# The last head group of a state space layer: gates first, its pairs moved amid another group's output, and the splits behind the transposes put first

## The chip, the cores and the metric

The kernel runs on one NeuronCore of a Trainium2 chip. The metric is device time of one execution in microseconds (us); lower is better. The kernel before takes 1437.23 us, the median of three runs (1435.54 to 1437.54).

## The reference

A two-layer encoder over 512 tokens of width 1024, in float32. The layer that the change touches is the second one, whose token mixer is a bidirectional state space scan:

```python
def ssd_mixer(hn, w_in, conv_w, conv_b, dt_bias, a_log, d_skip, norm_g, w_out):
    z, xbc, dt_raw = split(hn @ w_in)
    xbc = silu(depthwise_conv_centered(xbc, conv_w, conv_b))
    xs, bm, cm = split(xbc)
    dt = softplus(dt_raw + dt_bias)                   # per token, direction and head
    log_a = dt * -exp(a_log)
    y = bidir_scan(cm, bm, xs * dt[fwd], xs * dt[bwd], log_a[fwd], log_a[bwd])   # chunks of 128
    y = y + xs * d_skip
    y = y * silu(z)                                   # the gate
    yg = y by group (4 groups of 512 columns)
    yg = yg * rsqrt(mean(yg * yg) + EPS)              # RMS norm within the group
    return (yg * norm_g) @ w_out
```

In `bidir_scan` each head (32 heads of 64 columns, 8 to a group) needs a 128 x 128 matrix of decays per chunk, `exp` of differences of cumulative sums, times `c b` of its group. The layer then does `x = x + rms_norm(m)`, `hn = rms_norm(x)`, and a GeGLU feed-forward of which the up-projection comes first (`hn @ w_up`).

## The kernel before, in words

Every float32 matrix product is made as three products of a "high" and a "low" part (`mm3`, L86 to L88): `xh`, `whi`, `yh`, `hh` are high parts, rounded by a copy on ScalarE (L81); `xl`, `wlo`, `yl`, `hl` are low parts, the difference, made on VectorE (L82). Weights arrive by DMA into `wst` and are split there. PSUM holds the products (`mm`).

The state space layer, `mixer1`, goes through its four groups in the order of the strings `SLOTS`, one per group. A step is a letter and a number:

- `t6` to `t9` and `n..`: a projection tile of this or of the next group (24 matmuls of 128x512). Tiles 6 to 9 are the gates `z`; `S` and `N` apply silu to whatever has been projected since (L689, L692). The tiles 0 to 5 of a group are silu'd one group earlier.
- `G`: the products `pg` of the group, copied to `gt`. `s`: states of the scan. `h0` to `h7` (`head`): the decays `e` of one head, from two rows broadcast by DMA (`pb`). L741 makes the forward exponent on ScalarE, L742 the backward one and the maximum of both on VectorE, in four pieces of 128x128; L744 makes the step sizes `ds`; then `exp` over 128x512 (L745) and two products (L746, L747).
- `i0` to `i3` (`inter`): the part of `y` that comes through the states (`pi`, `ti`) and the skip.
- `p0` to `p3` (`pair`): the part within the chunks of two heads (`py`, L782), then on VectorE `y` plus `py` (L785) and `y` times the gate (L786), the square `sq` on ScalarE (L788), its running sum on GpSimd (L792), and the split `yh`, `yl` (L794, L795) for the output projection.
- `o0`, `o1` (`out`): the output projection of the group before, four tiles of 12 matmuls each. `r` (`rms`): the mean squares of a group, as matmuls `pss`, and their power `rg` on GpSimd.

The last group has no next group whose work could be laid between its steps. After its string come the output projection of the last group itself (two tiles first, then `pss`, then the other six), and `TAIL`: for each 128 tokens `t`, `fin` makes `m` (L828), a sum of squares (`junk`, L119) and `mg` (L150); x0 to x3 add the normalised `m` to `x` (L175); s0 to s3 make `xs` (L131), and t0 to t3 (`turn`) transpose it (`pt`, L140) and split it into `xh` and `xl`, with which the feed-forward's up-projection starts, first for half the tokens (`mm<-xh,whi 128x256`), two column tiles for each. `out_tile` for the last group also reloads `x` from a copy `xd` in DRAM (L829). The third column tile's weights are `hh` and `hl`, cast into memory that the pools of `mixer1` free.

A scheduler fixes the order on each engine from the program order; `high_priority` pulls instructions ahead, and `issue_after` keeps the silu group together. Each engine runs its list in order. An instruction that waits holds back all behind it on its engine.

Of the kernel before, what the change touches and what calls it, by code (L numbers as in the profile page):

```python
# [7 lines left out]
F32 = mybir.dt.float32  # L8
R32 = mybir.dt.float32r
BF16 = mybir.dt.bfloat16  # L10
AF = mybir.ActivationFunctionType
ALU = mybir.AluOpType
# [3 lines left out]
P = 128  # L16
S = 512
NT = S // P
# [7 lines left out]
class Env:  # L26
# [107 lines left out]
    def turn(self, t):  # L134

        nc = self.nc
        for h, xs in enumerate(self.xs[t]):
            pt = self.px.tile([P, 4, P], F32, name="pt", tag="px")
            for j in range(4):
                nc.tensor.transpose(pt[:, j], xs[:, j * P:(j + 1) * P], self.ident)  # L140
            o = (slice(None), slice(h * 4, h * 4 + 4), slice(t * P, (t + 1) * P))
            self.split(self.xh[o], self.xl[o], pt)
# [155 lines left out]
def mixer0(E, w0, w_v, w_fm, tabs, dist_d, logit, gn, bias, w_out, g_post_row, done):  # L298
# [235 lines left out]
NG = 4  # L534
# [18 lines left out]
def mixer1(E, w_dt, w_fm, cw, dtc, cols, mask, w_out, g_post_row, done):  # L553
# [5 lines left out]
    C = P  # L559
    H, H2 = SSD_H, 2 * SSD_H  # L560
    with ExitStack() as ctx:
# [20 lines left out]
        ddt = one.tile([P, NT, H], F32, name="ddt")  # L582
        etot = one.tile([P, H2, NT], F32, name="etot")
# [3 lines left out]
        def steps():  # L587
# [64 lines left out]
            nc.vector.tensor_tensor(ddt, tok[:, 1, :, :H], tok[:, 1, :, H:], op=ALU.subtract)  # L652

# [76 lines left out]
        def head(o, j):  # L730

            g = o["g"]
            h = g * HPG + j
            pb = [three.tile([P, S], F32, name="pb", bufs=3) for _ in range(2)]
            for dr in range(2):
                nc.sync.dma_start(pb[dr], pd[dr * H + h].partition_broadcast(P))
            e = three.tile([P, NT, C], F32, name="e")
            ds = ys.tile([P, NT, C], F32, name="ds")
            for c in range(NT):
                cc = slice(c * C, (c + 1) * C)  # L740
                nc.scalar.activation(e[:, c], pb[0][:, cc], AF.Identity, scale=-1.0, bias=tok[:, 0, c, h:h + 1])  # L741
                nc.vector.scalar_tensor_tensor(e[:, c], pb[1][:, cc], tok[:, 0, c, H + h:H + h + 1], e[:, c],  # L742
                                               op0=ALU.subtract, op1=ALU.max)
                nc.scalar.activation(ds[:, c], um, AF.Identity, scale=ddt[:, c, h:h + 1], bias=tok[:, 1, c, H + h:H + h + 1])  # L744
            nc.scalar.activation(e, e, AF.Exp, scale=-1.0)  # L745
            nc.vector.tensor_tensor(e, e, o["gt"], op=ALU.mult)  # L746
            o["m"][j] = e, nc.vector.tensor_tensor(e, e, ds, op=ALU.mult)  # L747

        def inter(o, q):
# [8 lines left out]
            for dr in range(2):  # L758
# [8 lines left out]
                if dr == 0:  # L767
                    nc.vector.tensor_scalar(y[:, :C], x[:, :C], d, None, op0=ALU.mult)
# [5 lines left out]
        def pair(o, q):  # L774
# [13 lines left out]
            nc.scalar.activation(sq, y, AF.Square)  # L788
            if q == 0:
                o["sq"] = sq  # L790
            else:
                nc.gpsimd.tensor_tensor(o["sq"], o["sq"], sq, op=ALU.add)  # L792
            yh, yl = four.tile([P, S], R32, name="yh"), four.tile([P, S], R32, name="yl")
# [4 lines left out]
        def rms(o):  # L798

            pss = E.px.tile([P, NT], F32, name="pss", tag="px")  # L800
            for c in range(NT):
                nc.tensor.matmul(pss[:, c:c + 1], o["sq"][:, c * C:(c + 1) * C], mean, start=True, stop=True)
# [13 lines left out]
        def out_tile(o, n, t, ws, fin=None, ps=None):  # L816
# [9 lines left out]
            else:  # L826
                m = three.tile([P, 512], F32, name="m", tag="e")
                nc.vector.scalar_tensor_tensor(m, ps, r, acc, op0=ALU.mult, op1=ALU.add)  # L828
                nc.sync.dma_start(acc, xd[t, :, ns])  # L829
# [7 lines left out]
        gs = [dict(g=g, t={}, st={}, m={}, yi={}, y=[], silu=[]) for g in range(NG)]  # L837
# [46 lines left out]
        def fin(t, n, m):  # L884
# [3 lines left out]
        xt = two.tile([P, 4, 512], R32, name="wo", tag="xt")  # L888
        ws = [E.wunit(w_out[NG - 1, 0, 0]) + E.wunit(w_out[NG - 1, 0, 1]),
              E.wunit(w_out[NG - 1, 1, 0], t4(one, ("state00", "state10", "state01", "state11"))) + E.wunit(w_out[NG - 1, 1, 1], [xt[:, i] for i in range(4)])]  # L890
# [152 lines left out]
```

## Time and profile before

| | |
|---|---|
| median of three runs | 1437.23 us (1435.54 to 1437.54) |
| the profiled execution | 1435.78 us, of which the span in the trace is 1434.0 us |
| TensorE (PE) busy | 98% of the span |
| VectorE (DVE) busy | 66% |
| ScalarE (ACT) busy | 50% |
| GpSimd (POOL) busy | 4% |
| mean granted TensorE clock | 0.996 of full speed |

The span is cut into what each engine did and waited for. PE's share is nearly full, so the places where PE is idle are the ones to look at. Times in a timeline are counted from the start of the span. In that view a row is a run of equal instructions, so a count like x16 covers 16 records; the float32 products that are not split (`py`, `pi`, `pss`, `pt`) have two records for each matmul.

### The profile page before, as it was taken

Reading aid. Unit: us, or ns where it says so; the run is one execution under the profiler, and the core shown is the slowest. Engines: PE = TensorE matmul, PEld = TensorE weight load, DVE = VectorE, ACT = ScalarE, POOL = GpSimd, SP = SyncE. Lnnn points to the kernel's source line nnn. Section 1 sums busy time; section 2 is a strip of 40 time slices with the busy share of each in tenths; the row PEclk is TensorE's granted clock in tenths of the full one; section 3 lists DMA queues with packets and bytes.
Section 4 is the critical chain, followed back from the end, with each engine's and each line's share of the span. In section 5 each row is a group of like instructions: output and inputs, shape, how many; then the busy total and the mean of one; then the engine's idle time right before and its main releaser. Section 6 shows DMA issues by size and latency. Waiting matters only on the chain.

```text
span 1434.0 us, 18009 instructions
## 1 busy us (share of the span) xinstructions
PE 1398.5 (98%) x6832; PEld 1141.0 (80%) x6832; DVE 946.3 (66%) x1486; ACT 720.3 (50%) x1192; POOL 60.6 (4%) x67
## 2 busy tenths in 40 slices
PE   7999999999999999999999999999889999999998
PEld 6877777898888888888777787777678888888886
DVE  7368888666566552357889786999886666564242
ACT  5356665454444431334888766577544444443230
POOL 0010110100000000000000000000110000000000
PEclk9999999999999999999999999999999999999999
DMA  7443232233233333332556354345432233333241
GB/s 255 146 141 92 85 96 77 83 108 102 89 98 95 102 94 97 120 107 95 159 180 184 111 176 131 95 153 162 143 120 87 90 100 94 100 89 102 89 132 59
DMA packets 56950, 166.34 MB, mean 116 GB/s; under 512 B 7200, under 2 KB 7968, under 8 KB 56864
## 3 DMA queue, kind: packets, MB, share of 16 engines
q1 hardware_dynamic: 56864, 165.20, 37.2%
q8 instruction: 54, 0.88, 0.2%
q14 instruction: 32, 0.26, 0.1%
HBM read 157.57 MB, written 5.51 MB: 114 GB/s over the span
## 4 chain that ended last, share of the span: by engine, by line
PE 80%; DVE 9%; ACT 5%; DMA 3%; issue 2%; POOL 0%; SPq 0%; DVEq 0%; POOLq 0%; ACTq 0%
PE mm L86 24%; PE mm L87 24%; PE mm L88 24%; DMA pb<-pd 1%; DVE wlo L82 1%; PE st L719 1%; DVE xf L683 1%; PE pt L140 1%; PE y L449 1%; PE pi L762 1%; DMA wst<-in_c_out 1%; PE pt L663 1%; PE py L782 1%; DVE ti L766 1%; DVE yl L795 0%
## 5 line engine op out<-in xcount | busy, mean ns | idle before, releaser
L88 PE MATMUL mm<-xl,whi 128*128 128x512 f32 (+2 forms) x1216 | 463.9, 382 | 4.0 <-DVE xl L82 3.8
L86 PE MATMUL mm<-xh,whi 128*128 128x512 f32 (+2 forms) x1216 | 464.0, 382 | 1.5 <-ACT z L689 0.7
L87 PE MATMUL mm<-xh,wlo 128*128 128x512 f32 (+2 forms) x1216 | 463.4, 381 | 1.4 <-DVE wlo L82 1.4
L82 DVE TENSOR_TENSOR wlo<-wst,whi 128x1024 fp32r<-128x1024 f32 (+1 forms) x208 | 255.5, 1229 | 198.0 <-ACT whi L81 195.8
L81 ACT CAST whi<-wst 128x1024 fp32r<-128x1024 f32 (+1 forms) x208 | 217.3, 1045 | 191.4 <-PE mm L87 119.6
L88 PEld LDWEIGHTS mm<-xl,whi 128*128 128x128 f32 (+1 forms) x1216 | 228.6, 188 | 48.4 <-DVE xl L82 4.5
L86 PEld LDWEIGHTS mm<-xh,whi 128*128 128x128 f32 (+1 forms) x1216 | 229.0, 188 | 46.8 <-issue 2.4
L87 PEld LDWEIGHTS mm<-xh,wlo 128*128 128x128 f32 (+1 forms) x1216 | 229.0, 188 | 45.2 <-DVE wlo L82 2.7
L227 DVE SCALAR_TENSOR_TENSOR cv<-mm,cwt,cv 128x511 f32<-128x511 f32 x88 | 65.7, 747 | 95.2 <-ACT cv L226 94.9
L86 PE MATMUL mm<-whi,hh 128*128 128x512 f32 x288 | 112.0, 389 | 0.0
L87 PE MATMUL mm<-whi,hl 128*128 128x512 f32 x288 | 112.0, 389 | 0.0
L88 PE MATMUL mm<-wlo,hh 128*128 128x512 f32 x288 | 112.0, 389 | 0.0
L226 ACT ACTIVATE cv<-mm,cwt 128x512 f32<-128x512 f32 x88 | 68.4, 777 | 39.8 <-PE mm L88 39.8
L81 ACT CAST hh<-cv 128x512 fp32r<-128x512 f32 x44 | 27.3, 621 | 100.5 <-DVE cv L235 100.3
L233 ACT ACTIVATE cv<-cv 128x512 f32<-128x512 f32 x44 | 27.8, 633 | 85.2 <-DVE cv L228 85.2
L228 DVE SCALAR_TENSOR_TENSOR cv<-mm,cwt,cv 128x511 f32<-128x511 f32 x88 | 66.0, 750 | 3.0
L744 ACT ACTIVATE ds<-um,tok,ddt 128x128 f32<-128x128 f32 x128 | 55.7, 484 | 16.1 <-DVE e L747 15.7
L88 PEld LDWEIGHTS mm<-wlo,hh 128*128 128x128 f32 x288 | 54.1, 188 | 11.3
L87 PEld LDWEIGHTS mm<-whi,hl 128*128 128x128 f32 x288 | 54.1, 188 | 11.2
L86 PEld LDWEIGHTS mm<-whi,hh 128*128 128x128 f32 x288 | 54.1, 188 | 11.2
L82 DVE TENSOR_TENSOR hl<-cv,hh 128x512 fp32r<-128x512 f32 x44 | 30.5, 693 | 28.9 <-ACT hh L81 28.9
L741 ACT ACTIVATE e<-pb,tok 128x128 f32<-128x128 f32 x128 | 43.0, 392 | 11.7 <-DMA pb<-pd 10.2
(236 smaller groups left out, 1945.6 us busy)
## 6 DMA issues: line engine op xcount, KB each, us to landing
wst<-in_f_up SPq DMA_DIRECT2D x88, 512.0 KB
wst<-in_f_down SPq DMA_DIRECT2D x44, 512.0 KB
wst<-in_c_fm SPq DMA_DIRECT2D x40, 512.0 KB
pb<-pd SPq DMA_DIRECT2D x64, 256.0 KB
wst<-in_ab_fm SPq DMA_DIRECT2D x20, 512.0 KB
gain<-yd SPq DMA_DIRECT2D x32, 256.0 KB
wst<-in_c_out SPq DMA_DIRECT2D x16, 512.0 KB
gain<-in_norms SPq DMA_DIRECT2D x8, 512.0 KB
```

The source lines that it names most:

```text
L81: self.nc.scalar.copy(hi, src)
L82: self.nc.vector.tensor_tensor(lo, src, hi.bitcast(F32), op=ALU.subtract)
L86: mm(out, lh, rh, start=first, stop=False)
L87: mm(out, ll, rh, start=False, stop=False)
L88: mm(out, lh, rl, start=False, stop=last)
L140: nc.tensor.transpose(pt[:, j], xs[:, j * P:(j + 1) * P], self.ident)
L226: nc.scalar.activation(o, ps, AF.Identity, scale=w(1), bias=w(3))
L227: nc.vector.scalar_tensor_tensor(o[:, 1:], ps[:, :S - 1], w(0), o[:, 1:], op0=ALU.mult, op1=ALU.add)
L228: nc.vector.scalar_tensor_tensor(o[:, :S - 1], ps[:, 1:], w(2), o[:, :S - 1], op0=ALU.mult, op1=ALU.add)
L233: nc.scalar.activation(g, g, AF.Gelu_apprx_tanh)
L741: nc.scalar.activation(e[:, c], pb[0][:, cc], AF.Identity, scale=-1.0, bias=tok[:, 0, c, h:h + 1])
L744: nc.scalar.activation(ds[:, c], um, AF.Identity, scale=ddt[:, c, h:h + 1], bias=tok[:, 1, c, H + h:H + h + 1])
```

## The change

- The string of the last group is rewritten: the gates `t9 t8 t6` come right after `G`, with the first three silu'd by one `S` and the fourth (`t7`) by another; the output tiles `o0` and `o1` of group 2 move from the front to places between the pairs `p0`, `p1`, `p2`.
- In `head`, for the last group only, the backward exponent is made on ScalarE with the bias `ntok` (minus the column of `tok`), in place in `pb`, and VectorE takes one maximum over 128x512 in place of four pieces.
- In `inter`, for the last group, the skip of the first 128 columns is made on ScalarE.
- In `pair`, the square of the last pair is not added on GpSimd; `pss` sums the two squares in PSUM. The split `y` of the pairs 0 and 1 goes into a tile `yx`; the last output weights take other buffers in turn.
- `x<-xd` is issued from ScalarE's queue, not from SP's.
- The splits behind the transposes are put at high priority, everywhere in the program.

```diff
@@ turn
-            self.split(self.xh[o], self.xl[o], pt)
+            with self.tc.high_priority(100):
+                self.split(self.xh[o], self.xl[o], pt)
@@ SLOTS, last group
-    "t9 G h0 s0 s1 o0 t8 h4 s2 h2 i0 t6 o1 t7 S h1 h3 p0 i1 p1 i2 i3 h5 p2 h6 h7 p3",
+    "G h0 s0 s1 t9 h1 t8 s2 i0 t6 S h2 t7 p0 i1 S h3 o0 p1 i2 h4 h5 o1 p2 i3 h6 h7 p3",
@@ steps
+            nc.vector.tensor_scalar(ntok, tok[:, 0, :, H:], -1.0, None, op0=ALU.mult)
@@ head
-                nc.vector.scalar_tensor_tensor(e[:, c], pb[1][:, cc], tok[:, 0, c, H + h:H + h + 1], e[:, c],
-                                               op0=ALU.subtract, op1=ALU.max)
+                if g < NG - 1:
+                    nc.vector.scalar_tensor_tensor(e[:, c], pb[1][:, cc], tok[:, 0, c, H + h:H + h + 1], e[:, c],
+                                                   op0=ALU.subtract, op1=ALU.max)
+                else:
+                    nc.scalar.activation(pb[1][:, cc], pb[1][:, cc], AF.Identity, bias=ntok[:, c, h:h + 1])
...
+            if g == NG - 1:
+                nc.vector.tensor_tensor(e, e, pb[1].rearrange("p (c l) -> p c l", c=NT), op=ALU.max)
@@ inter
-                    nc.vector.tensor_scalar(y[:, :C], x[:, :C], d, None, op0=ALU.mult)
+                    if g == NG - 1:
+                        nc.scalar.activation(y[:, :C], x[:, :C], AF.Copy, scale=d)
+                    else:
+                        nc.vector.tensor_scalar(y[:, :C], x[:, :C], d, None, op0=ALU.mult)
@@ pair
-            nc.scalar.activation(sq, y, AF.Square)
+            w = nc.scalar.activation(sq, y, AF.Square)
             if q == 0:
-                o["sq"] = sq
+                o["sq"] = [sq]
+            elif q == 3 and o["g"] == NG - 1:
+                o["sq"].append(sq)
             else:
-                nc.gpsimd.tensor_tensor(o["sq"], o["sq"], sq, op=ALU.add)
-            yh, yl = four.tile([P, S], R32, name="yh"), four.tile([P, S], R32, name="yl")
+                w = nc.gpsimd.tensor_tensor(o["sq"][0], o["sq"][0], sq, op=ALU.add)
+            o["sqw"].append(w)
+            if o["g"] == NG - 1 and q < 2:
+                if q == 0:
+                    o["yx"] = two.tile([P, 4, S], R32, name="yx", tag="xt")
+                yh, yl = o["yx"][:, 2 * q], o["yx"][:, 2 * q + 1]
+            else:
+                yh, yl = four.tile([P, S], R32, name="yh"), four.tile([P, S], R32, name="yl")
@@ rms
-                nc.tensor.matmul(pss[:, c:c + 1], o["sq"][:, c * C:(c + 1) * C], mean, start=True, stop=True)
+                for i, sq in enumerate(o["sq"]):
+                    E.together([nc.tensor.matmul(pss[:, c:c + 1], sq[:, c * C:(c + 1) * C], mean, start=i == 0,
+                                                 stop=sq is o["sq"][-1])], o["sqw"][2:])
@@ out_tile, last group
-                nc.sync.dma_start(acc, xd[t, :, ns])
+                nc.scalar.dma_start(acc, xd[t, :, ns])
@@ last output weights
-        xt = two.tile([P, 4, 512], R32, name="wo", tag="xt")
-              ... E.wunit(w_out[NG - 1, 1, 1], [xt[:, i] for i in range(4)])]
+              ... E.wunit(w_out[NG - 1, 1, 1], t4(four, ("yh", "yh", "yl", "yl")))]
```

What the lists of the engines look like at three places.

TensorE at the last pairs of the last group, before (`pi`, `py`: parts of a pair; `mm<-whi,yh` and `mm<-wo,yh`: the last group's output):

```order
L88 MATMUL mm<-xl,whi 128x512
L762 MATMUL pi<-cf,state_8334 128x128
L762 MATMUL pi<-cf,state_8469 128x128
L782 MATMUL py<-e,xt 64x128 x16
L86 MATMUL mm<-whi,yh 128x512
L86 MATMUL mm<-wo,yh 128x512
L87 MATMUL mm<-whi,yl 128x512
```

The last two pairs stand together behind the last gate's projection (`mm<-xl,whi`), and the output of the last group behind both. Now:

```order
L87 MATMUL mm<-wo,yx 128x512
L88 MATMUL mm<-wo,yx 128x512
L793 MATMUL py<-e,xt 64x128 x8
L822 MATMUL pss<-mean,sq 128x1 x8
L86 MATMUL mm<-whi,yh 128x512 x2
L86 MATMUL mm<-wo,yh 128x512
L87 MATMUL mm<-wo,yl 128x512
```

The last pair (`py`, x8) stands behind the halves of the last group's output that need the other pairs alone (`yx`), and `pss` follows it with nothing between.

VectorE in the tail, around the second 128 tokens, before (`m`, `mg`, `x`: the third and fourth 128 tokens; `xs`: transposed by TensorE; `xl`: the low part behind the transposes):

```order
L131 SCALAR_TENSOR_TENSOR xs_9037<-x_97,r_x_9035,gain_8969 128x512
L131 SCALAR_TENSOR_TENSOR xs_9039<-x_97,r_x_9035,gain_8969 128x512
L82 TENSOR_TENSOR wlo_9211<-wst_9208,whi_9210 128x1024
L109 TENSOR_SCALAR v_m_9083<-ssm0_9058,ssm1_9079 128x1
L828 SCALAR_TENSOR_TENSOR m_9127<-mm_9114,rg_8945,x_97 128x512
L175 SCALAR_TENSOR_TENSOR x_97<-mg_9057,r_m_9085,x_97 128x512
L175 SCALAR_TENSOR_TENSOR x_97<-mg_9078,r_m_9085,x_97 128x512
L150 TENSOR_TENSOR mg_9130<-m_9127,gain_8881 128x512
L828 SCALAR_TENSOR_TENSOR m_9148<-mm_9135,rg_8945,x_97 128x512
L109 TENSOR_SCALAR v_x_9092<-ssx_9089 128x1
L82 TENSOR_TENSOR xl_99<-pt_9173,xh_98 128x4x128
```

Eight instructions stand between `xs` and `xl`. Now:

```order
L82 TENSOR_TENSOR wlo_9224<-wst_9221,whi_9223 128x1024
L849 SCALAR_TENSOR_TENSOR m_9140<-mm_9127,rg_8958,x_97 128x512
L109 TENSOR_SCALAR v_x_9046<-ssx_9043 128x1
L849 SCALAR_TENSOR_TENSOR m_9161<-mm_9148,rg_8958,x_97 128x512
L131 SCALAR_TENSOR_TENSOR xs_9050<-x_97,r_x_9048,gain_8982 128x512
L131 SCALAR_TENSOR_TENSOR xs_9052<-x_97,r_x_9048,gain_8982 128x512
L151 TENSOR_TENSOR mg_9143<-m_9140,gain_8887 128x512
L151 TENSOR_TENSOR mg_9164<-m_9161,gain_8887 128x512
L82 TENSOR_TENSOR xl_99<-pt_9186,xh_98 128x4x128
L82 TENSOR_TENSOR xl_99<-pt_9193,xh_98 128x4x128
```

Two instructions are left between them, and `xs` now stands behind the `m` that reads the last output product (`mm_9148`).

VectorE and ScalarE at the fourth 128 tokens: first VectorE before, where `x` is complete (L175 twice) ahead of `hl`, with no split between:

```order
L82 TENSOR_TENSOR xl_99<-pt_9180,xh_98 128x4x128
L109 TENSOR_SCALAR v_m_9156<-ssm0_9131,ssm1_9152 128x1
L175 SCALAR_TENSOR_TENSOR x_97<-mg_9130,r_m_9158,x_97 128x512
L175 SCALAR_TENSOR_TENSOR x_97<-mg_9151,r_m_9158,x_97 128x512
L82 TENSOR_TENSOR hl_9216<-wst_9218,hh_9214 128x512
```

Now on VectorE:

```order
L109 TENSOR_SCALAR v_m_9169<-ssm0_9144,ssm1_9165 128x1
L176 SCALAR_TENSOR_TENSOR x_97<-mg_9143,r_m_9171,x_97 128x512
L82 TENSOR_TENSOR xl_99<-pt_9299,xh_98 128x4x128
L82 TENSOR_TENSOR xl_99<-pt_9306,xh_98 128x4x128
L176 SCALAR_TENSOR_TENSOR x_97<-mg_9164,r_m_9171,x_97 128x512
L82 TENSOR_TENSOR hl_9229<-wst_9231,hh_9227 128x512
```

And on ScalarE now, where the casts `xh` of the third 128 tokens stood behind `hh` and the following sum of squares before:

```order
L119 ACTIVATE junk_9166,ssm1_9165<-m_9161 128x512
L81 CAST xh_98<-pt_9299 128x4x128
L81 CAST xh_98<-pt_9306 128x4x128
L81 CAST hh_9227<-wst_9231 128x512
L81 CAST hh_9228<-wst_9231 128x512
L81 CAST hh_9237<-wst_9241 128x512
L81 CAST hh_9238<-wst_9241 128x512
L119 ACTIVATE junk_9176,ssx_9175<-x_97 128x1024
```

The split of the third 128 tokens now stands ahead of the second half of `x` on VectorE and ahead of `hh` on ScalarE.

## Rows read from the trace of the kernel before

**Rows 1.** The page: busy time, share of the span and instructions of each engine.

```profile
PE 1398.5 (98%) x6832; PEld 1141.0 (80%) x6832; DVE 946.3 (66%) x1486; ACT 720.3 (50%) x1192; POOL 60.6 (4%) x67
```

**Rows 2.** Timeline of PE, 1025 to 1041: start, length, instruction [idle before <-releaser].

```profile
1025.40 1.09 PE L782 MATMUL py<-e,xt 128*64 128x128 f32 x16 [3.69 <-DVE ti L766]
1026.87 1.97 PE L782 MATMUL py<-e,xt 128*64 128x128 f32 x16 [0.37 <-DVE ti L766]
...
1030.76 0.50 PE L87 MATMUL mm<-whi,yl 128*128 128x512 f32 x1 [0.59 <-DVE yl L795]
...
1038.04 0.50 PE L87 MATMUL mm<-whi,yl 128*128 128x512 f32 x1 [0.55 <-DVE yl L795]
...
1040.77 0.95 PE L802 MATMUL pss<-mean,sq 128*128 128x1 f32 x8
```

**Rows 3.** Timeline of ACT, 981 and 1021 to 1024.

```profile
981.05 1.27 ACT L741 ACTIVATE e<-pb,tok 128x128 f32<-128x128 f32 x4
...
1021.01 1.14 ACT L81 CAST wo<-wst 128x512 fp32r<-128x512 f32 x2 [1.39 <-DMA wst<-in_c_out]
1022.17 1.28 ACT L689 ACT_TABLE_LOAD   x1
1023.47 0.60 ACT L689 ACTIVATE z<-mm 128x512 f32<-128x512 f32 x1
```

**Rows 4.** Stretches of 20 us: length, busy of each engine, PEclk, DMA share, GB/s.

```profile
980.00:1000.00 20.00, 20.00 (x88) 15.38 (x88) 19.76 (x36) 14.20 (x31) 0.00 (x0) 1.00 0.58 170
1000.00:1020.00 20.00, 20.00 (x125) 16.40 (x124) 18.28 (x35) 13.28 (x31) 0.00 (x0) 1.00 0.52 156
1020.00:1040.00 20.00, 14.38 (x77) 10.30 (x76) 16.99 (x24) 10.30 (x16) 5.07 (x3) 0.91 0.44 137
```

**Rows 5.** Two short stretches in the same view (PE, PEld, DVE, ACT, POOL, PEclk, DMA).

```profile
1026.60:1030.00 3.40, 3.01 (x18) 2.10 (x18) 3.25 (x5) 2.81 (x4) 1.62 (x1) 0.50 0.75 220
1064.20:1067.60 3.40, 3.26 (x16) 2.97 (x15) 2.75 (x6) 0.00 (x0) 0.54 (x1) 0.50 0.31 97
```

**Rows 6.** Waits of PE, 950 to 1080: us in total, times, longest.

```profile
PE pt L140 <- DVE xs L131: 1.6, 2, 0.8
```

**Rows 7.** Timeline of PE in the tail, 1063 to 1075.

```profile
1063.67 0.39 PE L88 MATMUL mm<-xl,whi 128*128 128x256 f32 x1 [3.83 <-DVE xl L82]
...
1070.82 1.04 PE L140 MATMUL pt<-head,xs 128*128 128x128 f32 x8
1071.61 0.36 PE L86 MATMUL mm<-xh,hh 128*128 128x256 f32 x1
...
1074.56 1.04 PE L140 MATMUL pt<-head,xs 128*128 128x128 f32 x8
```

**Rows 8.** Timeline of DVE in the tail.

```profile
1062.93 0.68 DVE L82 TENSOR_TENSOR xl<-pt,xh 128x512 fp32r<-128x512 f32 x1
...
1067.06 1.41 DVE L175 SCALAR_TENSOR_TENSOR x<-mg,r_m,x 128x512 f32<-128x512 f32 x2 [0.65 <-POOL r_m L111]
...
1072.71 1.41 DVE L131 SCALAR_TENSOR_TENSOR xs<-x,r_x,gain 128x512 f32<-128x512 f32 x2 [0.66 <-POOL r_x L111]
```

**Rows 9.** Timeline of ACT in the tail.

```profile
1068.63 2.18 ACT L81 CAST hh<-wst 128x512 fp32r<-128x512 f32 x4 [4.58 <-issue]
1070.71 1.06 ACT L119 ACTIVATE junk<-x 128x1024 bf16<-128x1024 f32 x1
```

**Rows 10.** Groups by line and form, 950 to 1080: count, busy us, mean ns, idle before.

```profile
L742 DVE SCALAR_TENSOR_TENSOR e<-pb,tok,e 128x128 f32<-128x128 f32 x39 | 10.9, 343 | 0.0
...
L175 DVE SCALAR_TENSOR_TENSOR x<-mg,r_m,x 128x512 f32<-128x512 f32 x8 | 5.7, 748 | 0.7 <-POOL r_m L111 0.7
...
L82 DVE TENSOR_TENSOR xl<-pt,xh 128x512 fp32r<-128x512 f32 x8 | 5.3, 682 | 0.0
...
L786 DVE TENSOR_TENSOR y<-y,z 128x512 f32<-128x512 f32 x5 | 3.4, 686 | 0.9 <-ACT z L689 0.5 <-ACT z L692 0.3
...
L788 ACT ACTIVATE sq<-y 128x512 f32<-128x512 f32 x5 | 3.2, 632 | 5.5 <-DVE y L786 5.5
```

**Rows 11.** Timeline of SP's queue: one DMA issue.

```profile
1043.84 0.33 SPq L829 DMA_DIRECT2D x<-xd  x1
```

More of the change, by code (lines that the diff above doesn't have):

```diff
@@ L582, in mixer1 @@
         ddt = one.tile([P, NT, H], F32, name="ddt")
+        ntok = one.tile([P, NT, H], F32, name="ntok")
         etot = one.tile([P, H2, NT], F32, name="etot")
@@ L835, in out @@
                 out_tile(o, n, t, ws)
-        gs = [dict(g=g, t={}, st={}, m={}, yi={}, y=[], silu=[]) for g in range(NG)]
+        gs = [dict(g=g, t={}, st={}, m={}, yi={}, y=[], silu=[], sqw=[]) for g in range(NG)]
         def tiles(o, *ii):
@@ L887, in mixer1 @@
         t4 = lambda pool, tags: [pool.tile([P, 512], R32, name="wo", tag=t) for t in tags]
-        xt = two.tile([P, 4, 512], R32, name="wo", tag="xt")
         ws = [E.wunit(w_out[NG - 1, 0, 0]) + E.wunit(w_out[NG - 1, 0, 1]),
-              E.wunit(w_out[NG - 1, 1, 0], t4(one, ("state00", "state10", "state01", "state11"))) + E.wunit(w_out[NG - 1, 1, 1], [xt[:, i] for i in range(4)])]
+              E.wunit(w_out[NG - 1, 1, 0], t4(one, ("state00", "state10", "state01", "state11"))) + E.wunit(w_out[NG - 1, 1, 1], t4(four, ("yh", "yh", "yl", "yl")))]
         first = [out_mm(gs[-1], 0, ws[n]) for n in range(2)]
```

## The prediction

> **What bounds the kernel now.** I read the page first: TensorE is busy 98% of the span, no other engine over 66% [rows 1]. A change can win only where TensorE stands idle or runs at half speed, and in the part of the program that the change moves there are two such places. I found them in TensorE's timeline, then asked the timelines of VectorE and ScalarE who was late.
>
> The first is the last pairs of the last group. TensorE waits 3.69 us, then 0.37 us, with VectorE's `ti` named [rows 2]. `ti` was only queued behind a product with the gate; behind it stands ScalarE, which after its casts loads its function table (1.28 us at 1022.17) and makes the first gate at 1023.47 [rows 3]. The gates were projected last, so their silu came last. After that idle time the granted clock is 0.50, the lower level of 1.2 GHz, for 3.4 us [rows 5]; TensorE was busy 3.01 us of them, so half of that, 1.5 us, is lost. Two waits for `yl` follow, 0.59 and 0.55 us [rows 2].
>
> The second is the tail. TensorE waits twice for `xs`, 1.6 us together [rows 6], and 3.83 us for `xl`, which VectorE starts only at 1062.93 [rows 7, 8]. The clock falls again, to 0.50 for 3.4 us with 3.26 busy: 1.6 us lost [rows 5].
>
> Removable at most: 3.69 + 0.37 + 1.5 + 0.59 + 0.55 = 6.7 us in the first place and 1.6 + 3.83 + 1.6 = 7.0 us in the second, 13.7 us together.
>
> **The change part by part.** I count the waits that are taken away and the waits that the new order makes.
>
> *Gates first.* The four gates are now silu'd some 25 us earlier, beside projections and output tiles that do not need them. I take the 4.06 us of idle time, its half-speed stretch and the two `yl` waits as gone: −6.7 us. What is late next is the last pair, which is now alone before `pss`.
>
> *pss behind the last pair.* In the new list `pss` follows the last `py` with nothing between. From `py` to `pss` lie two VectorE products of the kind of L786 (0.686 each) and the square (0.632) [rows 10]: 2.0 us in which TensorE has nothing in front. Before, 38 output matmuls stood there. No cover is left, so +2.0. The doubled `pss` adds four matmuls, as much again as the old set at 0.95 us busy [rows 2]; without the tail of the last one I take +0.8.
>
> *The work moved to ScalarE.* 32 small activations, by a run of four at 1.27 us [rows 3] 0.32 us each, are 10.2 us, and the silu in two sets brings three more table loads, at 1.28 us 3.8 us: 14 us more. VectorE loses 32 x 0.343 and gains 8 x 0.686 us [rows 10]: 5.5 us less. ScalarE was busy 14.2 + 13.3 + 10.3 = 37.8 of 60 us from 980 to 1040 [rows 4]; now some 52 of 60. That is still no bound by itself, but ScalarE's list is in order and its waits for `pb` and for weights come on top, and the exponent of the last head stands near its end. So the last `py` can wait for `e`. Bounds: 0, if ScalarE keeps up, and 4.06 us, as long as this `py` waited before [rows 2]. I take 1.5, nearer to the lower end, since 8 us of slack are left. The Trainium skill speaks against this part: its page "ScalarE: Activation LUTs" (What ACT_TABLE_LOAD costs) gives about 1283 ns for the load and about 1380 ns more for a drain, 2.66 us at each switch. Here the casts end at 1022.15, the load starts at 1022.17 and the silu at 1023.47 [rows 3], so a switch costs 1.30 us, and no second part shows. By the page the three loads would cost ScalarE 8.0 us, the last `py` would be at its 4.06, and the whole sum 2.6 us worse; I go by the row.
>
> *Other new waits of the first place.* The first output tiles of the last group need the third pair's split and casts of weights: 0 to 1.2 us (two waits as long as those for `yl`), I take 0.6, one of them. The earlier group's `pss`, whose square ScalarE now makes a little later, and a weight split: 0 to 1.2 by the same rows, I take 0.4, since the output tiles that stood there remain in part.
>
> *Splits first in the tail.* `xl` of the second 128 tokens now has two instructions between `xs` and itself where there were eight. The chain from transposes to matmul is a cast (2.18 / 4 = 0.55 [rows 9]) and `xl` (0.682 [rows 10]), some 0.25 us of it beside the first high parts: +1.0 in place of 3.83, and the clock keeps up (−1.6). But the same order puts `xs` behind the `m` that reads the very last output product: `m` and `xs` are VectorE instructions of L175's kind, 0.748 each [rows 10], so TensorE waits 1.5 us at the least from its last product to the transposes; with the hand-over I take 1.6. Bounds: 0.8, as one of the two waits was [rows 6], and 2.2 if the sums of squares on ScalarE run late. The ScalarE queue now holds the eight issues of `x<-xd`, 0.33 us each by SP's row [rows 11]; up to three stand in front of a sum of squares, and that is the difference between 1.6 and 2.2. The first 128 tokens need no wait any more. So the tail's 7.0 us become 2.6.
>
> *hh behind the splits.* Here is the price. The casts `hh` start when the last L175 ends (1067.06 + 1.41, `hh` at 1068.63) [rows 8, 9], since they take over memory of the layer. Before, this was over before TensorE asked for `hh` at 1071.61 [rows 7]. Now the split of the third 128 tokens stands ahead of the second half of the last L175. From the end of these transposes: cast 0.55, `xl` 0.68, L175 0.75, the first `hh` 0.55, in all 2.5, with hand-overs 2.6 us in which TensorE has nothing in front: +2.6. Then the sum of squares of the last 128 tokens stands behind all four `hh`. They end some 1.6 us after the first one; from the start of that sum to `xs` it took 2.0 us (1070.71 to 1072.71) [rows 8, 9], and `xs` 0.75, so the transposes start some 6.95 us after the ones before. The matmuls between take 2.95 us (1071.61 to 1074.56 [rows 7]) from 2.6 on, and end at 5.55: +1.4. One weight split on VectorE now stands between the two last `xl`: +0.5, partly covered.
>
> *What I cost at nothing.* Splits first at other layer changes and at the start: TensorE did not wait for `xl` there by the waits that I read, and the same instructions are issued; ±0.5. The skip on ScalarE: four small activations, within the 14 us. `ntok`: one small VectorE instruction, beside projections.
>
> **The sum.** First place: −6.7 + 2.0 + 0.8 + 1.5 + 0.6 + 0.4 = −1.4. Tail: −7.0 + 1.0 + 1.6 + 2.6 + 1.4 + 0.5 = +0.1. Together −1.3 us, on the profiled execution's 1435.78 us: 1434.5. That execution lies 1.45 us under the median of the runs, 1437.23, so I forecast 1435.9 us. (What a measurement of this kernel can tell from no change is about 0.2%, 2.9 us; the forecast lies within.)
>
> **The rivals.**
>
> *A: the new waits are covered.* If ScalarE keeps up, the last `py` and the output tiles wait for nothing (−2.5), the transposes wait only 0.8 (−0.8), and the last transposes find their `xs` ready (−1.4): −1.3 − 4.7 = −6.0, 1431.2 us. For it: 8 us of slack on ScalarE in the stretch. Against it: the order makes the 1.4 and the 1.6, and the order is certain.
>
> *B: TensorE's clock falls again, at new places.* The idle times of 3.69 and 3.83 us were followed by 3.4 us at half speed, those of 0.8 were not [rows 2, 5 to 7]. The wait for `hh`, 2.6 us, lies between; the wait for the last `py` and that for `pss` lie one `py` apart and come to 3.5 together. If both are long enough, 1.5 and 1.6 us come back. It decides from a wait of `py` near its upper bound, since it then adds its own 2.5 as well: −1.3 + 3.1 + 2.5 = +4.3, 1441.5 us. For it: ScalarE's long list. Against it: only the longer waits were seen to bring the clock down.
>
> *C: splits first does not do what it says.* If the sums of squares behind ScalarE's DMA issues make `xs` so late that the tail's wait is only moved from `xl` to `xs`, 3.83 us stay in place of 1.0 + 0.6 and the half-speed stretch stays: −1.3 + 2.2 + 1.6 = +2.5, 1439.7 us. For it: `xs` stands behind the last `m`. Against it: `x<-xd` issues are short.
>
> **How the numbers follow.** My forecast, −4.3 to +1.6 us around it by its bounds (1433 to 1438.5): 0.48, of which 0.10 faster, 0.35 same, 0.03 slower. A: 0.26, faster. B: 0.20, of which 0.19 slower and 0.01 same. C: 0.06, half same, half slower. So faster 0.36, same 0.39, slower 0.25. The range for 8 in 10 reaches from A's middle to B's: 1430.0 to 1441.5.
>
> **What would show it.** In the changed kernel's profile: the wait of `py` for `ti` is gone, and one for `e` or none is in its place; `pss` waits some 2 us for the last `sq`; the wait for `xl` in the tail is 1 us or less; a wait of 2.5 to 3 us of the matmuls with `hh` for ScalarE appears, and one of 1 to 2 us for the last `xs`; a switch of the table on ScalarE stays 1.3 us. Half-speed stretches would show in the clock of 20 us stretches there (0.91 in such a one before [rows 4]). The prediction is wrong if the wait for `hh` is missing, or if idle time at the last pair comes to more than 5 us.

## The result, and the profile after

The changed kernel takes 1441.07 us (median of 6 runs, 1439.97 to 1441.83) against 1436.03 us (6 runs, the three of above among them) of the kernel before: a ratio of 1.0042, 95% interval [1.0032, 1.0052]. It is slower by 5 us where I had forecast 1.3 us faster.

In the profiled execution the span is 1439.3 us. From the mean squares of the second group (group 1 by the code's count) to the last matmul it took 548.2 us before and takes 555.8 us now, 7.6 us more; the loss lies here. PE in the timeline, first the kernel before, then the changed one:

```profile
878.73 0.95 PE L802 MATMUL pss<-mean,sq 128*128 128x1 f32 x8
...
1426.90 0.39 PE L88 MATMUL mm<-hl,hh 128*128 128x512 f32 x1
```

```profile
876.41 0.95 PE L822 MATMUL pss<-mean,sq 128*128 128x1 f32 x8
...
1432.20 0.39 PE L88 MATMUL mm<-hl,hh 128*128 128x512 f32 x1
```

The 2.3 us by which the first 877 us were shorter are not shown to be the change's: in the fourteen profiles of this study that point lies anywhere from 875.9 to 881.3, and experiment 7 finds no effect there. Why the medians differ by 5.0 and this part of single profiles by 7.6 stays open to that extent.

What TensorE waited for in the changed kernel, 950 to 1090 (us in total, times, longest):

```profile
PE mm L86 <- ACT hh L81: 3.4, 1, 3.4
PE pt L140 <- DVE xs L131: 2.7, 2, 2.4
PE pss L822 <- issue: 2.2, 1, 2.2
PE py L793 <- DVE e L755: 1.9, 1, 1.9
PE pss L822 <- POOL sq L805: 1.8, 1, 1.8
PE mm L87 <- DVE wlo L82: 0.6, 1, 0.6
PE mm L86 <- ACT yh L813: 0.4, 1, 0.4
PE mm L87 <- DVE hl L82: 0.3, 1, 0.3
PE mm L87 <- DVE yl L814: 0.2, 1, 0.2
PE mm L88 <- DVE wo L82: 0.2, 1, 0.2
```

These are 13.7 us; the same view of before came to 11.8 us (4.1 + 3.8 + 1.6 + 1.1 + 0.9 + 0.3). The wait for the gates and that for `xl` [rows 2, 7] are gone, others have come or grown, and the waits alone make it 1.9 us slower. The doubled `pss` adds 1.0 us (1.92 against 0.95 at full speed). What is left of the 7.6 us can be TensorE's clock, which the experiments test. Four stretches of the changed kernel (length; PE, PEld, DVE, ACT, POOL busy; PEclk; DMA):

```profile
966.70:970.10 3.40, 3.40 (x9) 2.64 (x8) 1.54 (x2) 3.39 (x6) 1.81 (x1) 0.50 0.55 195
1035.00:1045.20 10.20, 8.46 (x28) 7.43 (x29) 4.13 (x8) 2.99 (x6) 1.47 (x1) 0.50 0.17 48
1062.30:1065.70 3.40, 3.39 (x17) 3.20 (x16) 2.66 (x6) 1.79 (x4) 0.54 (x1) 0.50 0.81 302
1076.00:1079.40 3.40, 3.40 (x19) 3.40 (x18) 2.62 (x6) 1.34 (x3) 0.54 (x1) 0.51 0.64 187
```

TensorE was busy for 18.65 us of them at the lower level, 1.2 GHz; by that count half of it, 9.3 us, is lost. Before there were two such stretches with 6.27 us busy [rows 5], 3.1 us by the same count, 6.2 us less. This makes 1.9 + 1.0 + 6.2 = 9.1 us, more than the 7.6 seen: the count is an upper bound, since a slow matmul in front of a later wait costs nothing. Each stretch begins at or right behind a new wait, as the timeline of PE shows:

```profile
965.25 1.05 PE L822 MATMUL pss<-mean,sq 128*128 128x1 f32 x8 [1.79 <-POOL sq L805]
...
1033.43 1.09 PE L793 MATMUL py<-e,xt 128*64 128x128 f32 x16 [1.95 <-DVE e L755]
1036.74 3.54 PE L822 MATMUL pss<-mean,sq 128*128 128x1 f32 x16 [2.22 <-issue]
...
1061.81 1.75 PE L140 MATMUL pt<-head,xs 128*128 128x128 f32 x8 [2.42 <-DVE xs L131]
...
1070.21 1.18 PE L140 MATMUL pt<-head,xs 128*128 128x128 f32 x8
1074.78 0.39 PE L86 MATMUL mm<-xh,hh 128*128 128x256 f32 x1 [3.39 <-ACT hh L81]
...
1080.10 0.60 PE L140 MATMUL pt<-head,xs 128*128 128x128 f32 x4
```

The reader is to see three things. The last pair's `py` and `pss` stand with idle time on both sides, and the doubled `pss`, 1.92 us at full speed (experiment 3), takes 3.54. The wait for `hh` is there, at 3.39 us. And between `hh` and the last transposes lie 5.3 us (1074.78 to 1080.10) for matmuls that took 2.95 before [rows 7].

ScalarE's table switches, in its timeline:

```profile
988.46 1.28 ACT L692 ACT_TABLE_LOAD   x1
989.76 0.60 ACT L692 ACTIVATE z<-mm 128x512 f32<-128x512 f32 x1
990.25 1.08 ACT L695 ACTIVATE z<-mm 128x512 f32<-128x512 f32 x2
991.35 1.28 ACT L753 ACT_TABLE_LOAD   x1
992.65 0.63 ACT L753 ACTIVATE e<-e 128x512 f32<-128x512 f32 x1
```

From load to first use it is 1.30 us again, as in [rows 3]. What the Trainium skill's page "ScalarE: Activation LUTs" (What ACT_TABLE_LOAD costs) adds to the load, some 1380 ns of drain, shows at none of these switches.

### The profile page after: what moved, and what is told of

Its sections match the earlier page's. It is cut to its first block, busy times and chain, and to the rows that moved or that the text cites. A ratio compares the mean times of both kernels' runs of the same rounds, so it can differ in the third digit from the quotient of the medians.

```text
span 1439.3 us, 18018 instructions
## 1 busy us (share of the span) xinstructions
PE 1403.4 (98%) x6840; PEld 1145.9 (80%) x6840; DVE 939.6 (65%) x1459; ACT 734.1 (51%) x1231; POOL 61.8 (4%) x66
## 4 chain that ended last, share of the span: by engine, by line
PE 78%; DVE 8%; ACT 7%; DMA 4%; issue 2%; POOL 1%; SPq 0%; DVEq 0%; POOLq 0%; ACTq 0%
PE mm L86 24%; PE mm L87 24%; PE mm L88 24%; DMA pb<-pd 2%; DVE wlo L82 1%; DVE xf L686 1%; PE pt L140 1%; PE y L450 1%; ACT ds L750 1%; PE st L722 1%; ACT e L744 1%; ACT whi L81 1%; DVE x L176 1%; PE pi L770 0%; PE sc L434 0%
## 5 line engine op out<-in xcount | busy, mean ns | idle before, releaser
L750 ACT ACTIVATE ds<-um,tok,ddt 128x128 f32<-128x128 f32 x128 | 57.2, 484 | 10.6 <-DVE e L755 10.2
```

## The experiments

Times below are medians; each ratio is to runs of the kernel before on the same chip, with its 95% interval. Theory 1: the loss is TensorE's clock, at the new waits. Theory 2: the waits alone. Theory 3: one part of the change alone is to blame.

| | kernel | us | ratio to before | us at half speed, 940 to 1100 |
|---|---|---|---|---|
| | before | 1434.8 to 1436.0 | | 6.8 |
| | changed | 1441.07 | 1.0042 [1.0032, 1.0052] | 20.5 |
| 1 | changed + 12 spare matmuls ahead of `pss` | 1438.88 | 1.0022 [1.0012, 1.0032] | 13.7 |
| 2 | changed, splits not first | 1439.71 | 1.0033 [1.0020, 1.0045] | 20.5 |
| 3 | changed, old string | 1434.75 | 0.9996 [0.9987, 1.0005] | 10.2 |
| 4 | before + splits first | 1438.51 | 1.0026 [1.0016, 1.0037] | 17.1 |
| 5 | changed, old string, splits not first | 1435.47 | 0.9999 [0.9989, 1.0010] | 10.2 |
| 6 | as 5, splits first but for the tail | 1434.67 | 1.0000 [0.9991, 1.0009] | 6.8 |
| 7 | before + splits first but for the tail | 1434.70 | 0.9999 [0.9990, 1.0007] | 17.1 |
| 8 | changed + spare matmuls at four places | 1436.67 | 1.0011 [1.0001, 1.0021] | 3.4 |
| 9 | before + spare matmuls at two places | 1436.29 | 1.0009 [1.0001, 1.0018] | 3.4 |
| 10 | before + heads and skip on ScalarE | 1437.67 | 1.0022 [1.0011, 1.0034] | 20.5 |
| 11 | before + tile `yx`, weights in other buffers | 1435.17 | 1.0003 [0.9994, 1.0012] | 6.8 |
| 12 | as 6, `x` reloaded by SP | 1434.50 | 0.9999 [0.9989, 1.0008] | 13.6 |

The last column sums, over one profile each, the time at a granted clock of 0.50. It does not order the kernels by their time: 7 and 12 have 17.1 and 13.6 us and are level with before, 8 has 3.4 and is not faster than they are. It also differs between profiles of the same work. From group 1's `pss` to the end, number 7 has the order of the kernel before on all engines. Behind the same wait for the gates (3.57 us; before 3.69) its clock stays low for 10.2 us where it was 3.4 before [rows 5], and in the tail for 6.8:

```profile
1022.91 3.68 PE L786 MATMUL py<-e,xt 128*64 128x128 f32 x32 [3.57 <-DVE ti L770]
1022.00:1032.20 10.20, 8.88 (x44) 6.99 (x45) 9.86 (x17) 4.36 (x8) 1.78 (x1) 0.50 0.72 249
1059.60:1066.40 6.80, 4.84 (x22) 4.80 (x23) 6.05 (x11) 2.35 (x6) 1.08 (x2) 0.50 0.55 181
```

And yet that part takes 547.8 us, before 548.2. So 10 us more at half speed cost nothing at these places; what it costs has to be shown place by place.

**1. Spare matmuls between the last pair and the mean squares.**

```diff
+        junk = E.px.tile([P, 512], F32, name="warm", tag="px")
+        E.together([nc.tensor.matmul(junk, y0[:, :P], ws[0][0][0], start=True, stop=True) for _ in range(12)], [last py])
         rms(gs[-1])
```

> The changed kernel with 12 spare matmuls (128x512, result never read) between the last pair's products and the mean squares, where TensorE was idle 2.22 us. They only fill the idle time and keep TensorE active. Theory 1, the clock: the changed kernel is slower because TensorE ran at half speed four times (966.7 to 970.1, 1035.0 to 1045.2, 1062.3 to 1065.7, 1076.0 to 1079.4), not because of the waits alone. Then the stretch from 1035.0 shrinks to none or one of 3.4 us, and 2.5 to 4 us come back: 1437 to 1438.5 us against 1441.1. Theory 2, the waits alone: the spare matmuls cover a wait that ends when the square ends, nothing comes back, and the time stays at 1441 to 1442 us.

Measured 1438.88: 2.2 us of the 5 come back by work that computes nothing. In the profile a stretch of 3.4 us at half speed is left in place of 10.2. Theory 2 does not allow the gain. The size rests on the medians alone: the profile is of an execution of 1442.43 us, where the stretch behind the wait for `hh` is 6.8 us long, and from group 1's `pss` to the end it is only 0.9 us shorter than the changed kernel's (554.9 against 555.8).

**8. Spare matmuls at four places.** The same with 8 ahead of the last `py`, 10 behind it, 10 ahead of the second 128 tokens' transposes and 14 ahead of `hh`.

```diff
+    def warm(self, n, after):
+        wp = self.px.tile([P, 512], F32, name="warm", tag="px")
+        self.together([matmul(wp, self.xh[:, 0, :P], self.xh[:, 0:4, :P], start=True, stop=True) for _ in range(n)], [after])
```

> The changed kernel with spare matmuls at four places where TensorE idled: 8 near the end of the last output halves ahead of the last pair, 10 between the last pair and the mean squares, 10 ahead of the second 128 tokens' transposes, 14 ahead of the first matmul with hh. All operands as changed, results never read. Theory 1, the clock: three of the four half-speed stretches (all but the one at 966) go, of which 8.5 + 3.4 + 3.4 us were busy, at 7.6 us lost; the spare matmuls cost some 1 to 2 us where they are longer than the wait: 1435 to 1437 us. Theory 2, the waits alone: 1441 us or more, since the waits end when VectorE and ScalarE end.

Measured 1436.67, 4.4 us under the changed kernel. Only the stretch at 966 is left (20 us stretches of this kernel; the column before the last two is PEclk):

```profile
960.00:980.00 20.00, 18.12 (x93) 13.62 (x93) 11.85 (x18) 17.03 (x35) 3.19 (x2) 0.91 0.35 113
...
1020.00:1040.00 20.00, 19.28 (x116) 14.41 (x115) 14.65 (x22) 11.68 (x24) 1.28 (x1) 1.00 0.47 145
1040.00:1060.00 20.00, 18.98 (x85) 14.61 (x84) 18.60 (x33) 8.44 (x19) 5.18 (x5) 1.00 0.40 123
1060.00:1080.00 20.00, 18.92 (x139) 17.35 (x140) 15.36 (x27) 9.98 (x19) 2.54 (x4) 1.00 0.34 120
```

That holds beyond this profile: the mean granted clock was 0.997 to 0.999 in the eleven executions of number 8, and 0.992 to 0.993 in the six of the changed kernel. From group 1's `pss` to the end the profile takes 551.4 us, 4.4 less than the changed kernel's 555.8. Most of this comes between the last group's `pss` and the first transposes, 17.2 us in the changed kernel (1036.74 to 1053.97) and 13.9 here, with 48 output matmuls between in both (the first transposes, `pt`, of the changed kernel, then `pss` and `pt` of number 8):

```profile
1053.97 1.29 PE L140 MATMUL pt<-head,xs 128*128 128x128 f32 x8 [0.30 <-DVE xs L131]
```

```profile
1038.09 1.92 PE L835 MATMUL pss<-mean,sq 128*128 128x1 f32 x16
1051.96 1.29 PE L142 MATMUL pt<-head,xs 128*128 128x128 f32 x8 [0.60 <-DVE xs L131]
```

Another 2.0 us come between the first matmul with `hh` and the last transposes (5.3 against 3.3). The stretch at 1062 gave back 0.5 (8.4 against 7.9 us from the second transposes to the third). Not all of it is the clock. The spare matmuls also moved a few instructions: VectorE now completes `x` ahead of `xl`, and the matmuls with `hh` start 0.5 us earlier behind the third transposes. With that said, this shows theory 1 for most of the loss. The change with most of its clock losses covered is still 0.11% slower than before, not ahead of it.

**2 and 4. The splits.** The high priority in `turn` taken out of the changed kernel, and put alone into the one before.

```diff
-            with self.tc.high_priority(100):
-                self.split(self.xh[o], self.xl[o], pt)
+            self.split(self.xh[o], self.xl[o], pt)
```

> The changed kernel without the high priority of the splits behind the transposes. Theory 1: the 3.4 us wait for hh and the 3.4 us at half speed behind it go (-3.4 -0.3 -1.7), the wait for xl of the second 128 tokens comes back at 2.5 to 4 us in place of none, and the half speed behind it stays: 1438 to 1441 us. Theory 3, the splits are right and the string of the last group is to blame: without them it gets slower still, 1442 to 1444 us.

> The kernel before with only the high priority of the splits behind the transposes. By my sum: the wait for xl (3.83) and its half speed (1.6) go, 1.0 stays, a wait for hh of 2.6 to 3.4 us comes with half speed behind it (1.7), and the last transposes wait 1.4 more: +0 to +2 us, 1436 to 1438 us. Rival, the splits alone are a gain and the loss is all in the last group: 1432 to 1434 us.

The splits alone make the kernel before slower by 0.26%, 3.3 us by the medians, which is more than the 0 to 2 us that I expected of them. From group 1's `pss` to the end, as above, the profiles differ by 4.0 us on the kernel before (548.2 to 552.2) and by as much on the changed one (551.8 to 555.8). But the splits act behind the last group's `pss`, and from there to the end they cost 3.4 us on the kernel before (386.1 to 389.6) and 1.7 on the changed one (393.8 to 395.5), near the medians' 3.3 and 1.4. The intervals of number 2 and of the changed kernel overlap.

The rest of the second 4.0 us is the clock, by chance. From group 1's `pss` to the last group's, number 2 has the order of the changed kernel on all engines and the same wait at group 2's `pss`, and yet no half speed behind it:

```profile
966.58 1.05 PE L821 MATMUL pss<-mean,sq 128*128 128x1 f32 x8 [1.78 <-POOL sq L804]
968.00:971.40 3.40, 3.40 (x16) 2.80 (x15) 1.56 (x2) 3.39 (x6) 1.83 (x1) 1.00 0.71 236
```

From there to the last group's `pss` it takes 69.7 us, the changed kernel 71.5: 1.8 us more, beside 1.7 by half of the 3.40 us busy at 966.7. So at this place half speed costs its full price, which number 8 left untested. The kernel before with splits first waits 3.4 us for `hh` and 4.0 us for `xs`, and no more for `xl`:

```profile
PE py L783 <- DVE ti L767: 4.0, 2, 3.7
PE pt L140 <- DVE xs L131: 4.0, 3, 2.4
PE mm L86 <- ACT hh L81: 3.4, 1, 3.4
```

So the wait for `xl` of 3.83 us is only exchanged for one for `hh` and a longer one for `xs`.

**3. The old string.**

```diff
-    "G h0 s0 s1 t9 h1 t8 s2 i0 t6 S h2 t7 p0 i1 S h3 o0 p1 i2 h4 h5 o1 p2 i3 h6 h7 p3",
+    "t9 G h0 s0 s1 o0 t8 h4 s2 h2 i0 t6 o1 t7 S h1 h3 p0 i1 p1 i2 i3 h5 p2 h6 h7 p3",
```

> The changed kernel with the old string of the last group, all else as changed. Theory 3, the new string is to blame (it put the last pair's chain bare before the mean squares and moved output tiles away from group 2's mean squares): 1436 us or less, with one half-speed stretch fewer than four. Theory 1 (every place where TensorE idles for some 2 us costs the clock): the wait for the last gate comes back with its 3.7 us and half speed, and the time stays within 1439 to 1443 us.

Measured 1434.75: with the old string the whole rest of the change is level with before. The new string is the largest cost, as theory 3 has it, by the way that theory 1 has it: it made the waits at 965, 1033 and 1036, and two of the four half-speed stretches, the long one among them, stand behind these. But theory 1 as stated for this run, that every idle time of some 2 us costs the clock and with it the time, failed: waits of 4.22 and 1.74 us and 10.2 us at half speed are left in the tail, and the kernel is level with before. With the old string, the rest of the change already cut the wait for the gates:

```profile
1019.63 1.09 PE L793 MATMUL py<-e,xt 128*64 128x128 f32 x16 [1.30 <-DVE ti L774]
1021.10 1.09 PE L793 MATMUL py<-e,xt 128*64 128x128 f32 x16 [0.38 <-DVE ti L774]
...
1031.62 1.92 PE L822 MATMUL pss<-mean,sq 128*128 128x1 f32 x16 [0.17 <-issue]
```

**5, 6 and 7. Do the two costs add up?** The old string without splits first, the old string with them outside the tail alone (a flag set to false ahead of the tail), and the kernel before with that flag.

```diff
-            with self.tc.high_priority(100):
+            if self.hot: with self.tc.high_priority(100):
...
+        E.hot = False          # ahead of the last group's output tiles
```

> The changed kernel with the old string and without the high priority of the splits: what is left are the head and skip on ScalarE, the square of the last pair summed in PSUM, the tiles yx and x reloaded from ScalarE's queue. From the end of group 1 to the end, the splits cost 4.0 to 4.1 us (changed against the one without the splits, 555.8 to 551.8; before with the splits against before, 552.3 to 548.2) and the new string 7.1 (555.8 against 548.7 with the old string). If both costs add up, this kernel is 3.5 us faster than before in that part: about 1432 us. If they share a half-speed stretch and do not add: 1434 to 1435.

> As the one before (old string), with the splits at high priority everywhere but in the tail of the state space layer. In four profiles with the splits the first 260 us were 1.2 us shorter on the mean than in two without. If that is an effect: 1 to 1.5 us under the kernel without any, 1430.5 to 1431 us. If it is scatter of single profiles: the same as the one before.

> The kernel before with the splits at high priority everywhere but in the tail of the state space layer. If the start gains by them: 1 to 1.5 us under the kernel before. If not: no difference.

All three are level with before. They do not add up: from group 1's `pss` to the end number 5 takes 547.3 us, 3 takes 548.7, before 548.2. (The 4.0 us for the splits were too much, as just said.) Of what is won at the gates nothing is left at the end. In number 5 `pss` starts 67.2 us behind the one of the group before (970.63 to 1037.82; before 968.12 to 1040.77, 72.7). Some 2 of these 5.5 us are output matmuls that now stand behind `pss` (187 split matmuls between the two `pss` where there were 196). But the second 128 tokens' transposes come 22.7 us behind `pss` (1060.48) where it was 17.0 before (1057.74):

```profile
1037.82 1.92 PE L821 MATMUL pss<-mean,sq 128*128 128x1 f32 x16 [0.18 <-issue]
...
1060.48 1.94 PE L140 MATMUL pt<-head,xs 128*128 128x128 f32 x8 [3.52 <-DVE xs L131]
```

In number 5, on VectorE, the last `yl` and the splits of the last output weights stand there between `pss` and the first `m`:

```profile
1039.78 0.16 DVE L824 TENSOR_SCALAR ss<-pss 128x4 f32<-128x4 f32 x1 [2.78 <-PE pss L821]
1039.86 0.75 DVE L813 SCALAR_TENSOR_TENSOR yl<-y,col,yh 128x512 fp32r<-128x512 f32 x1
1040.53 1.29 DVE L82 TENSOR_TENSOR wo<-wst,wo 128x512 fp32r<-128x512 f32 x2
1041.74 1.55 DVE L848 SCALAR_TENSOR_TENSOR m<-mm,rg,x 128x512 f32<-128x512 f32 x2
```

The chain of the tail runs over VectorE, ScalarE and GpSimd, and starting TensorE's part earlier does not end it earlier. The 1.2 us that profiles with splits first seemed to gain at the start are scatter, by number 7.

**9. Spare matmuls in the kernel before**, 16 at the gates and 17 behind the second 128 tokens' transposes, by `warm` as in 8.

```diff
+        if self.tail and t == 1:                    # behind the transposes in tr
+            self.warm(17, lastpt)
...
+            if o["g"] == NG - 1 and q == 2:         # behind the gates' products
+                E.warm(16, E.lastproj)
```

> The kernel before with 16 spare matmuls (128x512, results never read) where TensorE waits 3.69 us for the gates, and 17 behind the second 128 tokens' transposes, where it waits 3.83 us for xl. Nothing else is changed. Theory 1, the clock: both half-speed stretches of before go, 1.5 and 1.6 us come back, and the spare matmuls end about with the waits: 1432 to 1433 us against 1435.2. Theory 2, half speed costs nothing here because the work behind it waits for VectorE anyway: 1435 to 1436.5 us.

Measured 1436.29, slower by 0.09%, and at the gates it tests nothing: the spare matmuls needed a PSUM buffer that `ti` had to free, waited 3.52 us themselves and then stood in the way for 3.9 us:

```profile
1018.10 0.60 PE L769 MATMUL pi<-cf,state 128*128 128x128 f32 x4
1022.22 3.91 PE L149 MATMUL warm<-xh 128*128 128x512 f32 x16 [3.52 <-DVE ti L773]
```

In the tail the half-speed stretch is gone, but from the second 128 tokens' transposes to the last ones it took 17.3 us (1056.69 to 1074.03) against 16.8 before: the matmuls, now fast, wait for `xl` again, 1.45 and 0.86 us. There half speed had cost nothing, as number 7 shows too; the 1.6 us that I had listed as removable were VectorE's.

**10 and 11. Two parts of the change alone, on the kernel before.** In 10 the heads' second exponent and the skip on ScalarE; in 11 the tile `yx`, with the last weights in the buffers of `yh` and `yl`.

```diff
+                    nc.scalar.activation(pb[1][:, cc], pb[1][:, cc], AF.Identity, bias=ntok[:, c, h:h + 1])
...
+                        nc.scalar.activation(y[:, :C], x[:, :C], AF.Copy, scale=d)
```

```diff
+                    o["yx"] = two.tile([P, 4, S], R32, name="yx", tag="xt")
+                yh, yl = o["yx"][:, 2 * q], o["yx"][:, 2 * q + 1]
```

> The kernel before with the head's second exponent and the skip of the last group on ScalarE. With the old string and the whole rest of the change the wait for the gates was 1.30 + 0.38 us in place of 3.69 + 0.37. If the heads did that (VectorE relieved): 1.3 to 2 us here too, and 1432 to 1433 us. If the moved casts of output weights did it: the wait stays above 3 us, and ScalarE's longer list makes it no better, 1435 to 1438 us.

> The kernel before with the tile yx for the first two pairs and the last output weights in the buffers of yh and yl. Two of the four casts of output weights now stand behind the gate's silu on ScalarE. If they made the gates late: the wait falls to 1.3 to 2.5 us. But the split of these weights then stands on VectorE between the mean squares and the first m, 1.3 to 2 us, and the transposes of the tail come later: 1434 to 1437 us in all. If the casts do not matter: the wait stays at 3.7 us and the time at 1435 to 1437.

The heads alone make it slower, by 0.22%, and the wait for the gates stays (3.2 us); the last group's `pss`, which waited for nothing before, now waits 2.02 us for the sum of the squares. With `yx` the wait for the gates falls to 1.79 us, and the time stays. ScalarE in number 11:

```profile
1016.43 1.14 ACT L81 CAST wo<-wst 128x512 fp32r<-128x512 f32 x2 [2.54 <-DMA wst<-in_c_out]
1017.59 1.28 ACT L689 ACT_TABLE_LOAD   x1
1019.33 0.60 ACT L689 ACTIVATE z<-mm 128x512 f32<-128x512 f32 x1 [0.46 <-PE mm L88]
```

The silu now waits for its own product. Before, it stood behind a second pair of casts that waited 1.39 us for a weight DMA [rows 3]. That row was in the prediction, and I read it as "the gates came last". That is part of it; these casts and their DMA were another, since the wait falls by 1.9 of its 3.69 us without them.

**12. `x` reloaded from SP's queue.**

```diff
-                nc.scalar.dma_start(acc, xd[t, :, ns])
+                nc.sync.dma_start(acc, xd[t, :, ns])
```

> The changed kernel with the old string, the splits at high priority everywhere but in the tail, and x reloaded from SP's queue again. From the mean squares to the first xs it took 13.5 us without the splits' priority against 9.2 before. If the issues on ScalarE (0.33 us each, ahead of the sums of squares) are a part of it: that stretch falls by 0.7 to 1.5 us and the time to 1433 to 1434. If not: no difference to 1434.7.

No difference to number 6 (0.9999 [0.9989, 1.0008] and 1.0000 [0.9991, 1.0009]). The issues on ScalarE show no cost. None of the versions is clear of the kernel before on the fast side.

## Why the prediction was wrong

The waits came where the prediction has them, most of them larger than forecast, and they are most of what it worked out. Neither of its own signs of being wrong came: the wait for `hh` is there, and the idle time at the last pair is 4.2 us (1.95 + 2.22).

- *Gates first* took their wait away, as said.
- *pss behind the last pair*: 2.0 forecast, 2.22 measured. *The last py waits for e*: 1.5, 1.95. *Output operands*: 0.6, 0.7 (0.41 for `yh`, 0.17 for `yl`, 0.15 for `wo`). *The doubled pss*: 0.8, 1.0. *hh behind the splits*: 2.6, 3.39 and 0.34 more for `hl`. *xs behind the last m*: 1.6 with 2.2 as the upper bound, 2.42 and 0.30 more for the first 128 tokens. *xl in the tail*: 1.0, none.
- *Group 2's pss and a weight split*: 0.4 forecast; the waits were 1.79 and 0.6 where it had been 0.85 (`pss` of before), 1.5 more. I had kept "the output tiles that stood there remain in part"; in fact the matmuls that stand between the last `py` of group 2 and its `pss` fell from 18 to 13.
- *The last transposes' 1.4 us* did not come: the matmuls ahead of them ran at half speed and filled the time. With the clock up, in experiment 8, it is 0.30.

The step that failed is *the clock*, on both of its sides. The sum took 3.1 us of half speed away, as busy time by half, though nothing in the rows showed that these stretches held the kernel up. Where it was tested they did not: without the one in the tail experiment 9 gained nothing, and number 7, with 10 us more at half speed than before, is level. And the sum put no half speed in, on the ground that only idle times of 3.69 and 3.83 us had been followed by it and those of 0.8 had not. Between these ends there was no row, the change made five waits of 1.8 to 3.4 us, and I let the sum go with the lower end. The changed kernel was busy for 18.65 us at 0.50 there. Spare matmuls at three of the four stretches brought 4.4 of the 5.0 us back (experiment 8), and the fourth cost 1.8 (number 2). By half of the busy time the sum would have been −1.3 + 9.3 = +8.0, near the 7.6 of the profiles, but both of its clock terms are upper bounds.

Three smaller slips stand in the prediction's numbers. Rival C counts the wait for `xs` at 0.6 where the sum has 1.6, so it comes to +1.5 and not +2.5. The bound of +1.6 gives 1438.8, not 1438.5. And the range starts at 1430.0, which lies 1.2 below A's middle of 1431.2.

Rival B was the mechanism that decided, at the places it named (the last pair, `hh`) and two more. I gave it 0.20 and bound it to a wait of `py` near 4 us; here half speed began with 1.95 and 2.22 us on both sides of one `py`. That the measured +5.0 lies near B's +4.3 is in part luck: B's sum has the longest wait of `py`, which did not come, and 3.1 us for the clock. Of rival C a part came too: the wait for `xl` became one for `xs`, and a half-speed stretch stayed there, at 1062.3.

## What to carry to other kernels

A change that trades one long wait of TensorE for several of about 2 us can lose by it where the sum of the waits is equal: price each wait once by its length and once by the matmuls that may run at half speed behind it, and ask whether anything waits for these matmuls: where TensorE would wait again anyway, half speed costs nothing. Spare matmuls that read what is already there can tell the two prices apart, if their PSUM buffer is free when they are wanted and the order on the other engines stays. A half-speed stretch in one profile is not a property of the kernel: look at the clock of several executions. And where a tail's chain runs over VectorE and ScalarE, follow that chain to its end before counting what an earlier start of TensorE is worth.

## What the runs showed of the hardware

Neither the length of a wait nor the order of the work tells whether the clock falls. In the changed kernel 1.79 us ahead of `pss` were followed by half speed from 966.7 on; in number 2, with the same order and 1.78 us, they were not. In experiment 9 a wait of 3.52 us was not followed by it either (its profile has one stretch at half speed, from 1034 on, behind a wait of 2.52 us for `yh`). Nor is the length of a stretch fixed: behind the wait for the gates it was 3.4 us before and 10.2 in number 7. What decides is not shown.

What half speed costs depends on the place. The stretch at 966 cost 1.8 us; the longer stretches of number 7 cost nothing more than the shorter ones of before. The 91 executions of the kernel before that ran beside the experiments say the same: their mean granted clock goes from 0.993 (21 executions, median 1435.2 us) to 0.997 (17 executions, median 1434.8 us), and the time hardly follows.
